# A hybrid attention layer: attention output kept once in fp32 and split at its load, the last branch product tile by tile, score banks opened before the staging buffers

## The chip, the cores and the metric

The kernel runs on one core of a Trainium2 chip. The metric is the device time of one execution in microseconds, over three runs: 1683.67, 1685.21 and 1689.54, median 1685.21. Engines are called as in the profile: PE (matmul), PEld (its weight load), DVE (vector), ACT (scalar), POOL (GpSimd) and SP, which issues every DMA of this kernel in one order.

## The reference

One layer of a backbone: 1024 latent tokens and 256 context tokens of width 1024 go through one combined projection and two branches, gated linear attention (a) and differential attention (b). The branches are gated, merged and projected.

```python
def diff_attention(q1, q2, k1, k2, v, lam):      # 8 heads, blocks of 128 queries
        s1 = jnp.einsum('bhqd,bhkd->bhqk', qb1, k1).astype(jnp.float32) * scale
        s2 = jnp.einsum('bhqd,bhkd->bhqk', qb2, k2).astype(jnp.float32) * scale
        a = jax.nn.softmax(s1, axis=-1) - lam * jax.nn.softmax(s2, axis=-1)
        return jnp.einsum('bhqk,bhkv->bhqv', a.astype(v.dtype), v)
...
    a = merge_heads(rms_norm(o_gla) * gla_gain) * jax.nn.silu(gla_gate)
    b = merge_heads(rms_norm(o_diff) * diff_gain * (1 - lam_init)) * jax.nn.silu(diff_gate)
    y = jax.nn.sigmoid(m_gla) * (a @ w_br_gla) + jax.nn.sigmoid(m_diff) * (b @ w_br_diff)
    return y @ w_out
```

All of it is fp32. The kernel reaches that precision with two tensors for one: `hi`, a copy in the reduced format fp32r, and `lo`, what is left of the value. A product of two such pairs is three matmuls (`mm3`, L340): hi·hi, hi·lo, lo·hi.

## The kernel before

**Order.** The program is recorded by Python coroutines. Class `Driver` holds modelled times of the engines and runs the coroutine that is due first by time and priority; what it emits is the fixed order of instructions of PE, ACT, DVE and POOL, and SP issues the DMAs in the order in which they were recorded. So an edit of one coroutine can change the order of others. Buffers have tags with a count (`TAGS`, L231): `acq` takes one, `rel` gives it back when an instruction is done. A tag lies in a pool, and pools are opened and closed by stage, the next on the place of the last.

**Stages in the profile.** Projections and linear attention, to about 911 us (PSUM tiles mm, tp and others); differential attention, 911 to 1485; the rest of the branch products, to about 1606; the output product, to 1682.3; the last stores, to 1685.9.

**Opening of attention.** `to_b` waits until the tiles of five tags are idle (mm and tp in PSUM; w aside, the staging tiles p, pl and rope in SBUF), closes psA and sbA and opens psW, psB and sbB, which hold the score banks and attention's SBUF tiles.

**Attention.** For a head and a block of 128 queries: scores into a PSUM tile `s` of five banks, maxima on DVE (TENSOR_REDUCE, into `sm`), exponentials on ACT (`att_exp`, into `e`), the mix of the two softmaxes on DVE, transposes on PE through one of two PSUM banks `b1` (in the profile `b<-ident,e`), copies to SBUF and splits (`at`), and the product with v (`b<-at,vv`). Once for a head and a pair of blocks, 32 times in all, `att_fin` normalises the output, transposes it into a `b1` bank (`pb`), and splits it there: `hi` by ACT, `lo` by DVE, both read the bank, and the bank is given back behind `lo`. The two halves take two SBUF tiles `b1k` of five and are stored to `d_bT[0]` and `d_bT[1]`. `b<-ident,b1k` is the transpose, `b1k<-b` ACT's hi, and `b1k<-b,b1k` with output type fp32r is DVE's lo; `b1k<-b,b1k` with type f32 is another instruction of `att_fin`, a product of the first transpose with the gate, and holds the other bank.

**Fill.** Beside all this, `fill` runs the products that need no attention: gates (kind 0), a @ w_br_gla (kind 1, 8 tiles), and at the end b @ w_br_diff (kind 2, 8 tiles, PSUM tiles `mc`). A tile is 128 output channels; its weights are loaded (`raw`), split into two of four `wt` buffers (ACT hi, DVE lo), and it runs in two halves of 512 tokens, 24 matmuls each (8 k times 3). The right-hand operands are 16 buffers `h0` for the first half and 16 `h1` for the second. Tiles go in pairs: (n, half 0), (n+1, half 0), (n, half 1), (n+1, half 1). When the last pair of kind 1 has ended half 0, its 16 h0 buffers are given back, and `loads` fetches the 16 tiles hi and lo of half 0 of b from `d_bT` into them; half 1 follows likewise. The first two tiles of kind 2 go through `first_two`, whose four half tiles have their own banks: for half 0 it takes each k of both tiles in turn.

**Output product.** `left`, `right` and `stream` compute y @ w_out with seven products of quarter size. Operands of the left side are formed from y's tiles (`ya`, `yb`, `yc`, `yf`), those of the right side from w_out (`wr`, then `h<-wr`, or sums in `raw`, then `h<-raw`). y's half tiles are finished by `post_y`: DVE multiplies the PSUM tile by a gate into `o` and adds the other branch into `yf`.

Of the kernel before, what the change touches and what calls it, by code (L numbers as in the profile page):

```python
# [10 lines left out]
F32 = mybir.dt.float32  # L11
F32R = mybir.dt.float32r
# [216 lines left out]
class Hybrid:  # L229
# [160 lines left out]
    def scratch(self):  # L390
# [10 lines left out]
        self.d_aT = [[d(f"d_aT{j}{h}", [2, P, S]) for h in range(4)] for j in range(2)]  # L401
        self.d_bT = [[d(f"d_bT{j}{i}", [P, S]) for i in range(8)] for j in range(2)]
        self.d_m = [[d(f"d_m{j}{i}", [P, S]) for i in range(8)] for j in range(2)]
# [1432 lines left out]
    def att_exp(self, u, comp, s5):  # L1836
# [3 lines left out]
        yield d.on("DVE", mx)  # L1840
        self.dve.tensor_scalar(mx, mx, u["mt"][:, comp:comp + 1], None, ALU.min)
        yield from self.acq("e5")
        E = u["E"][comp] = self.t("e5", [P, T])
# [123 lines left out]
    def att_fin(self, hd, pr, po, zs):  # L1967
# [35 lines left out]
        yield AtPE(e)  # L2003
        yield from self.acq("b1k", 2)
        yield from self.acq("b1")
        pb = self.t("b1", [P, 2, P])
        for x in range(2):
            e = self.tr(pb[:, x], oo[:, x])
        self.rel("b1k", e)
        yield On(e, "ACT")  # L2010
        hi = self.t("b1k", [P, 2, P], F32R)
        lo = self.t("b1k", [P, 2, P], F32R)
        e = yield from self.split2(pb, hi, lo, "b1", self.SF)
        self.store([(self.d_bT[j][hd][:, pr * 256:(pr + 1) * 256], b.rearrange("p x t -> p (x t)")) for j, b in
                    enumerate((hi, lo))], ("b1k", 2), ("fin", 1), ev=self.ev_bT[hd] if pr == 3 else None)
        if (hd, pr) == (7, 3):
            self.d.set(self.ev_att)

    def fill(self):
# [80 lines left out]
        def loads(src, ready, prio=2):  # L2100
# [12 lines left out]
            return r  # L2113

        def pace(i):
            return self.ev_u[min(63, int(i * self.PACE))]
# [4 lines left out]
        while n < len(todo):  # L2121
            kind = todo[n][0]
            two = [x for x in (n, n + 1) if x < len(todo) and todo[x][0] == kind]
            end = all(t[0] != kind for t in todo[n + 2:])
            if kind == 2 and todo[n][1] == self.DT[0]:
                yield self.ev_c
                yield from self.first_two(evs[n:n + 2], (lambda: (ws[n], ws[n + 1])), rhs)
                n += 2
                continue
            for half in range(2):  # L2130
# [4 lines left out]
                if end:  # L2135
                    self.rel(f"h{half}", e, 2 * NK)
                    if half == 0 and kind == 0:
                        nxt = loads(lambda j, k: self.d_aT[j][k // 2][k % 2], [now] * NK)
                    if half == 0 and kind == 1:
                        nxt = loads(lambda j, k: self.d_bT[j][k], self.ev_bT)  # L2140
            n += len(two)
# [4 lines left out]
    def first_two(self, evs, ws, rhs):  # L2146
# [4 lines left out]
        for x in range(4):  # L2151
            yield from self.acq("mc")
            pms.append(self.t("mc", [P, 512]))
        for ev in evs:
            yield ev[0]
        for x in range(4):
            d.spawn(self.load_y(self.DT[x // 2], x % 2), prio=-1)

        for half, k, m in [(0, k, m) for k in range(NK) for m in range(2)] + [(1, k, m) for m in range(2) for k in range(NK)]:
            yield rhs.ev[k, half]  # L2160
            hi, lo = ws()[m]
            e = self.mm3(pms[2 * m + half], hi[:, k], lo[:, k], rhs[0][k][half], rhs[1][k][half], k == 0, k == NK - 1)
# [6 lines left out]
    def phase_b(self):  # L2169
# [8 lines left out]
        def to_b():  # L2178
            yield self.ev_stream
            yield self.ev_b2  # L2180
            yield from self.idle("mm", "tp", "p", "pl", "rope")
            self.close("psA", "sbA")
            self.open("psW", "psB", "sbB")
            yield self.ev_b2
            d.set(self.ev_b)

        d.spawn(to_b(), prio=-3)
        self.ev_k, self.ev_v = [Event() for _ in range(8)], [Event() for _ in range(8)]
        for g in (self.att_keys, self.att_queries, self.att_values):
# [274 lines left out]
```

## Time and profile before

| | us |
|---|---|
| median of three runs | 1685.21 |
| span of the profiled execution (its own time) | 1685.9 |
| to 911: PE busy | 891.03 of 911.00 |
| 911 to 1485: PE busy | 555.13 of 574.00 |
| 1485 to 1534.7: PE busy | 48.02 of 49.70 |
| 1534.7 to 1682.3: PE busy | 147.60 of 147.60 |
| behind it: last stores | 3.60 |

A row of the timeline reads: start, duration, engine, line, operation, output <- inputs, shape, count, and in brackets the engine's idle time ahead of it with what ended it. A line of a helper stands for all its callers (L197 for ACT, DVE and POOL, L335 for matmuls, L361 for transposes), so groups are told apart by their tiles. In the table of stretches the columns are named in its first row; PEclk is the granted clock of PE as a share of full speed, and DMA the busy share of the 16 DMA engines.

### The profile page before, as it was taken

Reading aid. Unit: us, or ns where it says so; the run is one execution under the profiler, and the core shown is the slowest. Engines: PE = TensorE matmul, PEld = TensorE weight load, DVE = VectorE, ACT = ScalarE, POOL = GpSimd, SP = SyncE. Lnnn points to the kernel's source line nnn. Section 1 sums busy time; section 2 is a strip of 40 time slices with the busy share of each in tenths; the row PEclk is TensorE's granted clock in tenths of the full one; section 3 lists DMA queues with packets and bytes.
Section 4 is the critical chain, followed back from the end, with each engine's and each line's share of the span. In section 5 each row is a group of like instructions: output and inputs, shape, how many; then the busy total and the mean of one; then the engine's idle time right before and its main releaser. Section 6 shows DMA issues by size and latency. Waiting matters only on the chain.

```text
span 1685.9 us, 24403 instructions
## 1 busy us (share of the span) xinstructions
PE 1641.8 (97%) x8389; PEld 1358.3 (81%) x8389; DVE 1167.5 (69%) x2035; ACT 788.4 (47%) x1624; POOL 601.7 (36%) x649
## 2 busy tenths in 40 slices
PE   8999999999999999999999999999999999999999
PEld 3788788888788888888878888888888787887887
DVE  4797853455578697687762988787787887525694
ACT  4666423343334535455442665556666555411231
POOL 1500200000156475465530446555565555700000
PEclk9999999999999999999999999999999999999999
DMA  8557947687683665645375344345368552279422
GB/s 305 167 205 258 325 164 248 226 282 273 200 258 114 197 203 169 207 134 169 117 196 154 85 128 132 104 116 138 113 169 245 167 157 67 98 234 337 151 100 75
DMA packets 255884, 302.84 MB, mean 180 GB/s; under 512 B 21480, under 2 KB 173968, under 8 KB 255760
## 3 DMA queue, kind: packets, MB, share of 16 engines
q1 hardware_dynamic: 255760, 301.29, 56.9%
q8 instruction: 66, 1.08, 0.3%
q14 instruction: 58, 0.48, 0.1%
HBM read 203.71 MB, written 97.52 MB: 179 GB/s over the span
## 4 chain that ended last, share of the span: by engine, by line
PE 43%; DVE 6%; ACT 2%; DMA 2%; POOL 2%; issue 2%; ACTq 0%; DVEq 0%; POOLq 0%; SPq 0%
PE mc L335 10%; PE mm L335 7%; PE mb L335 7%; PE s L335 6%; PE b L335 5%; DVE sm L197 3%; PE b L361 3%; POOL at L197 2%; DVE e L197 2%; PE go L335 1%; ACT e L197 1%; DMA h<-d_bT 1%; PE mz L335 1%; PE gs L335 1%; PE tp L361 1%
## 5 line engine op out<-in xcount | busy, mean ns | idle before, releaser
L335 PE MATMUL mm<-w,h 128*128 128x512 f32 x1260 | 319.3, 402 | 0.6 <-DVE w L197 0.4
L335 PEld LDWEIGHTS mm<-w,h 128*128 128x128 f32 x1260 | 232.0, 189 | 48.0 <-issue 1.0
L197 DVE TENSOR_REDUCE sm<-s 128x1 f32<-128x1024 f32 (+1 forms) x192 | 194.4, 1037 | 49.0 <-PE s L335 47.4
L335 PE MATMUL mb<-h,wt 128*128 128x512 f32 x744 | 204.5, 407 | 2.5 <-ACT ft L197 2.1
L197 ACT ACTIVATE e<-s,sm 128x1280 f32<-128x1280 f32 x128 | 169.9, 1330 | 68.0 <-DVE sm L197 60.3
L197 POOL TENSOR_TENSOR at<-ac,at 128x512 fp32r<-128x512 f32 x128 | 184.7, 1443 | 10.7
L197 POOL TENSOR_SCALAR at<-ac 128x512 fp32r<-128x512 f32 x128 | 100.6, 786 | 236.0 <-ACT ac L197 166.9
L335 PE MATMUL s<-hk,aq 128*128 128x512 f32 (+1 forms) x768 | 178.2, 365 | 3.2 <-ACT e L197 1.1
L335 PEld LDWEIGHTS mb<-h,wt 128*128 128x128 f32 x744 | 131.1, 190 | 25.9 <-ACT ft L197 3.6
L335 PE MATMUL mc<-h,wt 128*128 128x512 f32 x600 | 141.2, 392 | 1.7 <-DMA h<-d_bT 0.8
L335 PE MATMUL mm<-h,w 128*128 128x512 f32 x576 | 139.4, 398 | 2.7 <-ACT p L197 1.1
L335 PEld LDWEIGHTS s<-hk,aq 128*128 128x128 f32 x768 | 122.3, 190 | 23.9 <-ACT e L197 5.1
L335 PEld LDWEIGHTS mc<-h,wt 128*128 128x128 f32 x600 | 111.3, 188 | 26.9 <-DMA h<-d_bT 3.3
L335 PE MATMUL b<-at,vv 128*128 128x256 f32 x960 | 130.6, 285 | 0.5 <-POOL at L197 0.4
L335 PEld LDWEIGHTS mm<-h,w 128*128 128x128 f32 x576 | 108.6, 191 | 27.0 <-DVE h L197 1.4
L335 PEld LDWEIGHTS b<-at,vv 128*128 128x128 f32 x960 | 122.7, 190 | 5.6 <-POOL at L197 1.2
L197 POOL TENSOR_TENSOR sm<-sm,nhalf 128x2 f32<-128x2 f32 (+2 forms) x94 | 106.1, 1129 | 53.6 <-DVE sm L197 48.1
L197 DVE TENSOR_TENSOR w<-raw,w 128x512 fp32r<-128x512 f32 x120 | 92.5, 789 | 31.5 <-ACT w L197 30.3
L197 ACT ACTIVATE ac<-b 128x512 f32<-128x512 f32 x120 | 71.1, 600 | 84.9 <-PE b L361 79.7
L197 DVE SCALAR_TENSOR_TENSOR e<-e,sm,e 128x1280 f32<-128x1280 f32 x64 | 108.7, 1698 | 0.6
L197 ACT ACTIVATE w<-raw 128x512 fp32r<-128x512 f32 x120 | 72.5, 628 | 70.3 <-DVE raw L197 22.8
L361 PE MATMUL b<-ident,e 128*128 128x128 f32 x598 | 92.5, 276 | 12.4 <-DVE at L197 4.3
(283 smaller groups left out, 2832.5 us busy)
## 6 DMA issues: line engine op xcount, KB each, us to landing
raw<-in_w_in SPq DMA_DIRECT2D x63, 512.0 KB, 4.7
g<-d_s SPq DMA_DIRECT2D x32, 640.0 KB, 5.2
aq<-d_qT SPq DMA_DIRECT2D x128, 128.0 KB, 3.4
d_dv<-pl SPq DMA_DIRECT2D x40, 256.0 KB, 2.2
gv<-d_v SPq DMA_DIRECT2D x40, 256.0 KB, 3.2
d_kT<-pl SPq DMA_DIRECT2D x40, 256.0 KB, 3.0
hk<-d_kT SPq DMA_DIRECT2D x32, 320.0 KB, 5.7
vv<-d_dv SPq DMA_DIRECT2D x16, 640.0 KB, 6.2
```

Source lines behind the costliest of these rows:

```text
L197: self.ins = f(out, *args, **kw).ins
L335: self.ins = self.nc.tensor.matmul(out, lhsT, rhs, start=start, stop=stop, skip_group_check=more).ins
L361: self.nc.tensor.transpose(out, src, self.ident[:n, :n])
```

## The change

1. `att_fin` copies the transposed output once, by ACT, into one fp32 tile `bb`, and gives the bank back behind that copy. One `b1k` buffer is taken instead of two, one store of 128 KB is made instead of two, and `d_bT` has 8 tensors instead of 16.
2. `splits` takes the place of `loads` for kind 2: each of 16 operand tiles is loaded as fp32 into a staging tile `wr` (8 buffers of pool sbC, so behind `ev_c2`, the event that says that sbC is open), then split by ACT and DVE into two h buffers.
3. Tiles 6 and 7 of kind 1 and all of kind 2 run one by one, half 0 and half 1 of a tile in turn. `first_two` takes k 0 to 6 of the first tile, k 0 to 6 of the second, then k 7 of both, and waits for each tile's weights apart.
4. `to_b` opens the score banks when mm and tp are idle; sbA is closed and sbB opened when p, pl and rope are idle too, and `att_exp` waits for that with a new event `ev_sb`.

By count PE has 8075 rows in both orders; DVE goes from 2026 to 2010, ACT from 1381 to 1397, SP from 1008 to 960; POOL has the same.

```diff
-        self.d_bT = [[d(f"d_bT{j}{i}", [P, S]) for i in range(8)] for j in range(2)]
+        self.d_bT = [d(f"d_bT{i}", [P, S]) for i in range(8)]
...
         self.dve.tensor_scalar(mx, mx, u["mt"][:, comp:comp + 1], None, ALU.min)
+        yield self.ev_sb
         yield from self.acq("e5")
...
-        yield from self.acq("b1k", 2)
+        yield from self.acq("b1k")
         yield from self.acq("b1")
         pb = self.t("b1", [P, 2, P])
...
-        hi = self.t("b1k", [P, 2, P], F32R)
-        lo = self.t("b1k", [P, 2, P], F32R)
-        e = yield from self.split2(pb, hi, lo, "b1", self.SF)
-        self.store([(self.d_bT[j][hd][:, pr * 256:(pr + 1) * 256], b.rearrange("p x t -> p (x t)")) for j, b in
-                    enumerate((hi, lo))], ("b1k", 2), ("fin", 1), ev=self.ev_bT[hd] if pr == 3 else None)
+        bb = self.t("b1k", [P, 2, P])
+        self.rel("b1", self.act.activation(bb, pb, AF.Copy))
+        self.store([(self.d_bT[hd][:, pr * 256:(pr + 1) * 256], bb.rearrange("p x t -> p (x t)"))],
+                   ("b1k", 1), ("fin", 1), ev=self.ev_bT[hd] if pr == 3 else None)
...
+        def splits():
+            r = Rhs([[[None] * 2 for _ in range(NK)] for _ in range(2)])
+            r.ev = {(k, half): Event() for k in range(NK) for half in range(2)}
+
+            def one(k, half, x):
+                yield from self.acq(f"h{half}", 2)
+                hi, lo = (self.t(f"h{half}", [P, 512], F32R) for _ in range(2))
+                r[0][k][half], r[1][k][half] = hi, lo
+                yield d.on("ACT", x)
+                self.act.activation(hi, x, AF.Copy)
+                yield d.on("DVE", hi)
+                e = self.dve.tensor_tensor(lo, x, hi.bitcast(F32), ALU.subtract)
+                self.rel("wr", e)
+                d.set(r.ev[k, half], e)
+
+            def run():
+                yield self.ev_c2
+                for half in range(2):
+                    for k in range(NK):
+                        yield self.ev_bT[k]
+                        yield from self.acq("wr")
+                        x = self.t("wr", [P, 512])
+                        self.dma(x, self.d_bT[k][:, half * 512:(half + 1) * 512])
+                        d.spawn(one(k, half, x), prio=-2)
+            d.spawn(run(), prio=-2)
+            return r
...
-            two = [x for x in (n, n + 1) if x < len(todo) and todo[x][0] == kind]
-            end = all(t[0] != kind for t in todo[n + 2:])
+            one = kind == 2 or todo[n][:2] in ((1, 6), (1, 7))
+            two = [n] if one else [n, n + 1]
+            end = all(t[0] != kind for t in todo[n + len(two):])
             if kind == 2 and todo[n][1] == self.DT[0]:
                 yield self.ev_c
-                yield from self.first_two(evs[n:n + 2], (lambda: (ws[n], ws[n + 1])), rhs)
+                yield from self.first_two(evs[n:n + 2], (lambda m: ws[n + m]), rhs)
...
-                        nxt = loads(lambda j, k: self.d_bT[j][k], self.ev_bT)
+                        nxt = splits()
...
-        for ev in evs:
-            yield ev[0]
-        for x in range(4):
-            d.spawn(self.load_y(self.DT[x // 2], x % 2), prio=-1)
-
-        for half, k, m in [(0, k, m) for k in range(NK) for m in range(2)] + [(1, k, m) for m in range(2) for k in range(NK)]:
+        order = [(0, k, m) for m in range(2) for k in range(NK - 1)] + [(0, NK - 1, 0), (0, NK - 1, 1)]
+        for half, k, m in order + [(1, k, m) for m in range(2) for k in range(NK)]:
+            yield evs[m][0]
+            if k == 0:
+                d.spawn(self.load_y(self.DT[m], half), prio=-1)
             yield rhs.ev[k, half]
-            hi, lo = ws()[m]
+            hi, lo = ws(m)
...
-            yield from self.idle("mm", "tp", "p", "pl", "rope")
-            self.close("psA", "sbA")
-            self.open("psW", "psB", "sbB")
-            yield self.ev_b2
+            yield from self.idle("mm", "tp")
+            self.close("psA")
+            self.open("psW", "psB")
             d.set(self.ev_b)
+            yield from self.idle("p", "pl", "rope")
+            self.close("sbA")
+            self.open("sbB")
+            d.set(self.ev_sb)
```

Where rows move. First DVE in attention, around the 22nd of the 32 splits: `sm<-s` are maxima, `b1k<-b,b1k` reads a `b1` bank (the fifth row is the lo, the last the product with the gate). Before:

```order
L197 TENSOR_REDUCE sm_13607<-s_1691_8527 128x1
L197 TENSOR_REDUCE sm_13606<-s_1691_8527 128x2
L197 TENSOR_REDUCE sm_13608<-s_1691_8527 128x1
L197 TENSOR_SCALAR sm_13607<-sm_13607,sm_13606 128x1
L197 TENSOR_TENSOR b1k_13684<-b_2842_13679,b1k_13683 128x256
L197 TENSOR_SCALAR sm_13608<-sm_13608,sm_13606 128x1
L197 TENSOR_TENSOR b1k_13667<-b_2845_13692,b1k_13667 128x256
```

Now:

```order
L197 TENSOR_REDUCE sm_13516<-s_1691_8515 128x1
L197 TENSOR_REDUCE sm_13515<-s_1691_8515 128x2
L197 TENSOR_REDUCE sm_13517<-s_1691_8515 128x1
L197 TENSOR_SCALAR sm_13516<-sm_13516,sm_13515 128x1
L197 TENSOR_SCALAR sm_13517<-sm_13517,sm_13515 128x1
L197 TENSOR_TENSOR b1k_13547<-b_2819_13567,b1k_13547 128x256
```

The lo is gone; the product still stands behind the three maxima.

Then PE where kind 2 begins (`mc` is the PSUM tile, `h` the operand, `wt` the weights; a new `wt` number is a new tile or its lo half). Before:

```order
L335 MATMUL mc_15526<-h_2752_13266,wt_15409 128x512
L335 MATMUL mc_15560<-h_3210_15472,wt_15533 128x512
L335 MATMUL mc_15560<-h_3211_15474,wt_15533 128x512
L335 MATMUL mc_15560<-h_3210_15472,wt_15534 128x512
L335 MATMUL mc_15562<-h_3210_15472,wt_15596 128x512
L335 MATMUL mc_15562<-h_3211_15474,wt_15596 128x512
```

Now, from the first tile's k 6 (18 matmuls into it):

```order
L335 MATMUL mc_15465<-h_3203_15431,wt_15368 128x512
L335 MATMUL mc_15465<-h_3204_15432,wt_15368 128x512
L335 MATMUL mc_15465<-h_3203_15431,wt_15369 128x512
L335 MATMUL mc_15467<-h_3191_15419,wt_15483 128x512
L335 MATMUL mc_15467<-h_3192_15420,wt_15483 128x512
```

The second tile's weights are used behind 21 matmuls of the first instead of behind 3. ACT now does there:

```order
L197 ACTIVATE h_3191_15419<-wr_15395 128x512
L197 ACTIVATE h_3193_15421<-wr_15397 128x512
L197 ACTIVATE h_3195_15423<-wr_15399 128x512
L197 ACTIVATE h_3197_15425<-wr_15401 128x512
L197 ACTIVATE h_3199_15427<-wr_15403 128x512
L197 ACTIVATE wt_15483<-raw_15285 128x1024
L197 ACTIVATE h_3203_15431<-wr_15407 128x512
L197 ACTIVATE h_3201_15429<-wr_15405 128x512
```

These are the operands' copies k 0 to 4, the second tile's weights, then k 6 and k 5; before, this stretch held weights alone.

Last, DVE where the output product's first operands are formed (`o<-o,mc` and `yf<-o` finish a half tile of y, `raw<-raw,gbo` and `h<-raw,h` form an operand). Before:

```order
L197 TENSOR_SCALAR o_16127<-o_16127,mc_16126 128x512
L197 TENSOR_TENSOR yf_16159<-o_16127 128x512
L197 TENSOR_TENSOR raw_15947<-raw_15947,gbo_15381 128x512
L197 TENSOR_TENSOR raw_16059<-raw_16059,gbo_15381 128x512 x2
L197 TENSOR_TENSOR h_3346_16169<-raw_15947,h_3345_16168 128x512
```

Now:

```order
L197 TENSOR_SCALAR o_16055<-o_16055,mc_16054 128x512
L197 TENSOR_TENSOR yf_16087<-o_16055 128x512
L197 TENSOR_SCALAR o_16090<-o_16090,mc_16089 128x512
L197 TENSOR_TENSOR yf_16118<-o_16090 128x512
L197 TENSOR_TENSOR raw_15875<-raw_15875,gbo_15247 128x512
L197 TENSOR_TENSOR raw_15952<-raw_15952,gbo_15247 128x512 x2
L197 TENSOR_TENSOR h_3333_16128<-raw_15875,h_3332_16127 128x512
```

One half tile more of y is finished ahead of the operands.

More of the change, by code (lines that the diff above doesn't have):

```diff
@@ L2180, in to_b @@
             yield self.ev_b2
-            yield from self.idle("mm", "tp", "p", "pl", "rope")
-            self.close("psA", "sbA")
-            self.open("psW", "psB", "sbB")
-            yield self.ev_b2
+            yield from self.idle("mm", "tp")
+            self.close("psA")
+            self.open("psW", "psB")
             d.set(self.ev_b)
+            yield from self.idle("p", "pl", "rope")
+            self.close("sbA")
+            self.open("sbB")
+            d.set(self.ev_sb)
         d.spawn(to_b(), prio=-3)
+        self.ev_sb = Event()
         self.ev_k, self.ev_v = [Event() for _ in range(8)], [Event() for _ in range(8)]
```

## The prediction, made before the changed kernel was run

> **What bounds the kernel now.** I read the page first, then the busy times by stage, then the tensor engine's waits and its timeline in the two stages that the change touches.
>
> ```profile
> span 1685.9 us, 24403 instructions
> PE 1641.8 (97%) x8389; PEld 1358.3 (81%) x8389; DVE 1167.5 (69%) x2035; ACT 788.4 (47%) x1624; POOL 601.7 (36%) x649
> ```
>
> PE works 97% of the span; every other engine has room on the average. So only three things can move the end: a gap of PE, a lowered clock, or a different number of matmuls. The change leaves that number as it is (8075 rows on PE in both orders), so I look for gaps and clock, stage by stage: attention, the tail of the branch products, the output product.
>
> ```profile
> core 0: us, PE busy (x) PEld busy (x) DVE busy (x) ACT busy (x) POOL busy (x), PEclk, DMA share, GB/s
> 911.00:1485.00 574.00, 555.13 (x3325) 474.02 (x3325) 445.61 (x857) 331.58 (x680) 312.62 (x288) 0.99 0.46 130
> 1485.00:1534.70 49.70, 48.02 (x206) 37.44 (x203) 10.82 (x13) 4.63 (x5) 0.00 (x0) 1.00 0.93 300
> 1534.70:1682.30 147.60, 147.60 (x650) 121.94 (x650) 108.38 (x167) 38.62 (x62) 0.00 (x0) 1.00 0.44 147
> ```
>
> The output product (last row) has PE busy in all of it: nothing to gain, only to lose. Attention leaves PE idle for 574.00 − 555.13 = 18.9 us. In the tail DVE and ACT have little to do and DMA is nearly full (0.93). The waits of PE in attention, by what ended them (us in total, times, longest):
>
> ```profile
> engine line waited for: us in total, times, longest us
> PE b L361 <- DVE at L197: 4.3, 6, 1.6
> PE b L361 <- DVE sm L197: 3.4, 1, 3.4
> PE b L361 <- DVE b1k L197: 3.1, 5, 2.0
> ```
>
> The longest two, with what DVE did just before them:
>
> ```profile
> 1339.98 2.94 DVE L197 TENSOR_REDUCE sm<-s 128x1 f32<-128x1024 f32 x3
> 1342.96 0.41 DVE L197 TENSOR_TENSOR b1k<-b,b1k 128x256 fp32r<-128x256 f32 x1
> 1343.42 0.41 DVE L197 TENSOR_TENSOR b1k<-b,b1k 128x256 f32<-128x256 f32 x1
> 1343.52 0.85 PE L361 MATMUL b<-ident,e 128*128 128x128 f32 x6 [3.35 <-DVE sm L197]
> ...
> 1409.12 0.42 DVE L197 TENSOR_TENSOR b1k<-b,b1k 128x256 fp32r<-128x256 f32 x1
> 1409.69 0.45 PE L361 MATMUL b<-ident,e 128*128 128x128 f32 x1 [2.03 <-DVE b1k L197]
> ```
>
> The instruction with the fp32r output is the lo half of att_fin's split. It reads a PSUM bank b and is what gives that bank back. Both gaps end some 0.15 us after it (1342.96 + 0.41 to 1343.52; 1409.12 + 0.42 to 1409.69): PE stood because the two b1 banks were held, one by a lo queued behind three REDUCEs. The row "DVE sm" names the wrong instruction for the first. Each gap is followed by a lower granted clock, the eighth column:
>
> ```profile
> 1344.00:1350.00 6.00, 5.98 (x27) 4.80 (x26) 3.88 (x9) 4.08 (x9) 5.11 (x7) 0.72 0.34 113
> 1410.00:1420.00 10.00, 10.00 (x53) 8.28 (x51) 8.06 (x16) 6.59 (x13) 5.94 (x6) 0.85 0.19 67
> ```
>
> **Part 1: attention output kept as one fp32 tensor.** It takes 32 lo subtractions from DVE (13.3 us) and leaves the 32 ACT copies as they are, with another output type:
>
> ```profile
> L197 DVE TENSOR_TENSOR b1k<-b,b1k 128x256 fp32r<-128x256 f32 x32 | 13.3, 414 | 4.9 <-ACT b1k L197 4.9
> L197 ACT ACTIVATE b1k<-b 128x256 fp32r<-128x256 f32 x32 | 12.3, 385 | 28.2 <-PE b L361 26.8 <-DMA aq<-d_qT 1.0
> ```
>
> DVE's 13.3 us lie beside PE and are worth nothing by themselves; what counts is that a bank now returns after the ACT copy. The gaps ended by a lo are 3.35 and 2.03, and one of 0.20 at 1019 that I leave at that; their clock losses are 6.00 × (1 − 0.72) = 1.7 and 10.00 × (1 − 0.85) = 1.5. Upper bound of the gain: 3.35 + 2.03 + 1.7 + 1.5 = 8.6 us. Lower bound 0: at 1343.42 the other bank was held too, by the product b1k<-b,b1k (f32 output) that still sits behind the same REDUCEs in the changed order, so that the same wait could end 0.3 us later by another owner. I take half, **−4.3**, since one of the two banks is free early in either gap, but the order around them is written anew. One long gap with its clock costs 3.35 + 1.7 = 5.1; a reordering can add one as well as remove one, so the range gets ±5 here. The stores fall from 64 to 32 beside a DMA share of 0.46: 0.
>
> A rule speaks on the clock. The Trainium skill, "TensorE: Matmul & The Clock Gate", section "HAM oscillation — how this bites in real kernels", asks for no idle gaps of PE above about 3.4 us, so by it neither gap here would cost clock. The trace disagrees: gaps of 3.35 and 2.03 us stand ahead of clocks of 0.72 and 0.85, and the measurement decides. By the rule the removable sum would be 5.4 instead of 8.6, half of it 2.7, and the whole forecast 1.6 us later.
>
> **Part 2: the split at the load, and the tail tile by tile.** What the tail loses now:
>
> ```profile
> 1485.00 30.89 PE L335 MATMUL mc<-h,wt 128*128 128x512 f32 x135
> 1516.13 0.73 PE L335 MATMUL mc<-h,wt 128*128 128x512 f32 x2 [0.24 <-ACT wt L197]
> 1517.39 14.01 PE L335 MATMUL mc<-h,wt 128*128 128x512 f32 x59 [0.53 <-DVE wt L197]
> 1531.56 0.73 PE L335 MATMUL mc<-h,wt 128*128 128x512 f32 x2 [0.16 <-DMA h<-d_bT]
> 1532.58 1.77 PE L335 MATMUL mc<-h,wt 128*128 128x512 f32 x4 [0.29 <-DMA h<-d_bT]
> 1534.68 25.68 PE L335 MATMUL mc<-h,wt 128*128 128x512 f32 x112 [0.33 <-DMA h<-d_bT]
> 1534.68 82.35 PE mc L335 x362
> ```
>
> The last row, of the chain of waits, gives the undisturbed price: 82.35 / 362 = 0.2275 us a matmul. The first five runs of the timeline are 135 + 2 + 59 + 2 + 4 = 202 matmuls, 45.95 us at that price, and take 1534.68 − 1485.00 = 49.68: **3.7 us lost**, to weights that become ready late (1516, 1517) and to operands still landing (1531 to 1534). The weights:
>
> ```profile
> 1515.02 1.06 ACT L197 ACTIVATE wt<-raw 128x1024 fp32r<-128x1024 f32 x1 [4.38 <-PE mc L335]
> 1516.11 1.23 DVE L197 TENSOR_TENSOR wt<-raw,wt 128x1024 fp32r<-128x1024 f32 x1 [4.21 <-ACT wt L197]
> h<-d_bT SPq DMA_DIRECT2D x32, 256.0 KB, 6.1
> L197 ACT ACTIVATE h<-wr 128x512 fp32r<-128x512 f32 x8 | 5.0, 625 | 6.7 <-PE mb L335 6.5
> L197 DVE TENSOR_TENSOR h<-wr,h 128x512 fp32r<-128x512 f32 x8 | 5.5, 686 | 0.4 <-PE mb L335 0.4
> ```
>
> Removed: 32 loads of 256 KB (8.4 MB in a stage that moves 49.7 us × 300 GB/s = 14.9 MB). Added: 16 loads of 256 KB, 16 ACT copies of 0.625 (10.0 us) and 16 DVE subtractions of 0.686 (11.0 us), prices from the same forms elsewhere. ACT has 49.70 − 4.63 = 45 us free and DVE 39, POOL takes no part: they hide if they come in time. First half: five operands are split while the last branch tile's second half runs (24 × 0.2275 = 5.46 us; five copies 3.1 and the last subtraction 0.7 behind). When that tile ends, ACT does the second tile's weights, 1.06, then k6, k5, k7, 0.625 each; DVE follows: weights lo at 1.06 + 1.23 = 2.3, then k5 at 3.0, k6 at 3.7, k7 at 4.4. Needed: k5's lo by the 17th matmul, 16 × 0.2275 = 3.6; k6's 4.3; k7's after two times 21 matmuls, 9.6; the second tile's weights after 21, 4.8 (before: after 3, 0.7, and that is the wait of 1516). Every one is ready, two by only 0.6 us; without this cover each us that ACT or DVE is late is a us of PE. The loads may wait in staging tiles ahead of the buffers' release, so the operands' landing leaves the path. Bounds of the gain 0 to 3.7; I take **−3.4**, near the top, as 0.3 is left for a first load or weight still late.
>
> **Part 3: score banks opened early.** All engines' rows, and what each waits for, are the same in both orders at the opening and for some hundred PE rows behind it. The first score matmul
>
> ```profile
> 911.31 2.58 PE L335 MATMUL s<-hk,aq 128*128 128x512 f32 x12 [0.74 <-ACT p L197]
> ```
>
> keeps its wait on ACT's last p. The most that could be had is this 0.74, the most that can be lost is nothing, as no wait is added ahead of it: **0**.
>
> **Part 4: the output product's start.** Single tiles change the order in which half tiles end, so that before the output product's first operands DVE now finishes four half tiles' gates and sums where it finished three.
>
> ```profile
> 1605.98 11.04 PE L335 MATMUL mc<-h,ya 128*128 128x512 f32 x48
> 1606.10:1617.00 10.90, 10.90 (x50) 9.03 (x49) 10.83 (x19) 2.70 (x5) 0.00 (x0) 1.00 0.49 156
> 1617.00:1627.90 10.90, 10.90 (x50) 9.03 (x49) 9.78 (x17) 4.78 (x10) 0.00 (x0) 1.00 0.20 74
> 1627.90:1638.80 10.90, 10.90 (x50) 9.03 (x49) 10.72 (x18) 4.56 (x10) 0.00 (x0) 1.00 0.06 24
> 1600.85 0.68 DVE L197 TENSOR_TENSOR h<-raw,h 128x512 fp32r<-128x512 f32 x1
> ```
>
> DVE is full in the first pieces, with 0.07 + 1.12 + 0.18 = 1.4 us to spare in 33. Its last subtraction for these operands, the row at 1600.85, lies 4.5 us ahead of the first matmul; the extra work puts DVE some 5 us further behind, so that this cover is used up. Counted through the order, the first operand comes about 1 us ahead of its use, the next product's last about 1 us ahead or none. Bounds 0 and 2.6 (5 less the spare, less a us of margin); I take **+0.3**.
>
> **The sum.** −4.3 − 3.4 + 0 + 0.3 = −7.4. The profiled execution's span is 1685.9, the median of the runs 1685.21, closer than the 5.9 us over which those scatter; from the median this gives 1677.8, forecast **1678**. A measurement of this kernel tells 0.3% (5.1 us) from no change: faster is below 1680.2, slower above 1690.3.
>
> **The rivals.**
> - *The tail's gain alone.* In attention the bank held by the product f32 b1k<-b,b1k takes over both waits. For it: at 1343.42 it was the second holder, and 4.3 us of the listed waits, under "DVE at", come from other DVE work. Against it: PE needs one bank to go on, and the copy frees it early. 1685.2 − 3.4 + 0.3 = 1682; the same. Chance 0.22.
> - *The slower side: attention's new order makes more bank waits.* Without 32 lo's DVE puts its REDUCEs and products elsewhere; products still wait behind REDUCEs (0.98 each, the row at 1339.98), while 150 instead of 132 matmuls of fill remain when attention ends, so less fill was spent in covering gaps. Two more gaps like that at 1343.52 cost 2 × 5.1 = 10.1, with −3.4 of the tail 1692. It decides once PE's idle in attention is above 18.9 + 3.4. Chance 0.15.
> - *The backlog of DVE decides at the output product.* 2.6 us late instead of 0.3 there: 1680.2 or later, the same. Chance 0.05.
> - *The splits come late in the tail.* The 0.6 us of cover is gone if ACT takes copies in another turn or a load lands late; the 3.4 stay lost: 1681.2, and 1686 if a wait of 4.4 us, all the splits behind the last tile's end, is added. Chance 0.04.
>
> My forecast has 0.54, of it 0.50 below 1680.2 and 0.04 above. So faster 0.50; same 0.04 + 0.22 + 0.05 + 0.03 and 0.01 of the slower case, 0.35; slower 0.15. Its own range is 1672 to 1682. The whole range is **1671 to 1688**: below, the sum with 8.6 − 4.3 more and some for a removed gap elsewhere; above, the rivals but for the worse part of the slower one.
>
> **What will show it.** In the profile after: no PE wait in attention that ends with a b1k of DVE in fp32r, PE idle there near 14 and clocks of 1.00 around the former gaps; about 46 us for 202 tail matmuls, with no wait for h or wt above 0.3; the first s<-hk still behind ACT p; no wait for h in the output product. A total wait of PE in attention above 22 us proves part 1 wrong; a tail that still loses 3 us proves part 2 wrong.

## The result, and the profile after

The changed kernel takes 1675.18 us, the median of 6 runs (1673.55 to 1676.87); the kernel before, beside it, 1687.47 (6 runs, 1683.67 to 1689.54). The ratio is 0.993, with a 95% interval of 0.9914 to 0.9946: faster by 0.7%.

The head of the page of the changed kernel, and the busy times of the same stretches as before (of each, the columns of the table before):

```profile
span 1675.2 us, 24268 instructions
PE 1634.8 (98%) x8389; PEld 1354.1 (81%) x8389; DVE 1166.3 (70%) x2019; ACT 796.3 (48%) x1640; POOL 606.4 (36%) x649
```

```profile
911.00:1485.00 574.00, 559.12 (x3352) 477.15 (x3351) 436.86 (x828) 330.93 (x681) 315.85 (x288) 1.00 0.44 127
1485.00:1534.70 49.70, 49.70 (x221) 41.14 (x220) 27.56 (x40) 15.70 (x24) 0.00 (x0) 1.00 0.91 302
```

DVE and ACT are busier in the second stretch, as the splits now lie there (27.56 and 15.70 us), and PE has no gap in it. Of PE's timeline three places: attention's first score product, the first matmul behind attention, the first of the output product.

```profile
910.12 2.58 PE L335 MATMUL s<-hk,aq 128*128 128x512 f32 x12 [0.74 <-ACT p L197]
...
1474.07 121.33 PE L335 MATMUL mc<-h,wt 128*128 128x512 f32 x534
1595.23 11.04 PE L335 MATMUL mc<-h,ya 128*128 128x512 f32 x48
```

The row of 534 matmuls is one run without a wait; the next starts 121.16 us later, so a matmul costs 121.16 / 534 = 0.2269 us, of which the tables below use 0.2268. With that price the two profiles can be set side by side. Attention ends with more or less fill left to do (516 matmuls before, 534 now), so I add the price of what is left to the time from the first score product to the last transpose, and call that *attention at equal fill*. What the branch products behind attention take above their price is the *tail's loss*.

| place | before | after | difference |
|---|---|---|---|
| start of attention | 911.31 | 910.12 | −1.2 |
| attention at equal fill | 573.69 + 117.03 = 690.7 | 563.95 + 121.11 = 685.1 | −5.7 |
| tail's loss | 120.98 − 117.03 = 3.95 | 121.16 − 121.11 = 0.05 | −3.9 |
| from the output product's start to the end of the span | 79.9 | 80.0 | 0 |

Together −10.7, the difference of the spans; by the medians, taken beside each other, it is −12.3. The first row isn't the change's: the order up to there is the same, and over the profiles of this study it starts between 907.05 and 911.31. PE's waits in attention are now these:

```profile
PE s L335 <- ACT e L197: 4.2, 9, 1.2
PE b L361 <- DVE at L197: 3.5, 6, 0.9
PE b L361 <- ACT b1k L197: 1.7, 6, 0.4
PE b L361 <- DVE b1k L197: 1.3, 4, 0.6
```

The long gaps of 3.35 and 2.03 us are gone; score products now wait nine times for ACT's exponentials instead of three times. All listed waits from 911 to 1468 sum to 13.9 us, before to 18.2. The granted clock gains too: before, three of the 20 us slices of attention have 0.91, 0.97 and 0.95, a loss of 20 × 0.17 = 3.4 us; now every slice has 1.00.

### The profile page after: what moved, and what is told of

Read it like the earlier page. It is cut to its first block, busy times and chain, and to the rows that moved or that the text cites. A ratio compares the mean times of both kernels' runs of the same rounds, so it can differ in the third digit from the quotient of the medians.

```text
span 1675.2 us, 24268 instructions
## 1 busy us (share of the span) xinstructions
PE 1634.8 (98%) x8389; PEld 1354.1 (81%) x8389; DVE 1166.3 (70%) x2019; ACT 796.3 (48%) x1640; POOL 606.4 (36%) x649
## 4 chain that ended last, share of the span: by engine, by line
PE 43%; DVE 7%; ACT 3%; issue 2%; POOL 1%; DMA 1%; SPq 0%; ACTq 0%; DVEq 0%; POOLq 0%
PE mc L335 11%; PE mm L335 7%; PE mb L335 7%; PE s L335 6%; PE b L335 5%; DVE sm L197 4%; PE b L361 3%; ACT e L197 2%; DVE e L197 2%; PE go L335 1%; POOL at L197 1%; PE mz L335 1%; PE gs L335 1%; PE tp L361 1%; PE gt L335 1%
## 5 line engine op out<-in xcount | busy, mean ns | idle before, releaser
L197 POOL TENSOR_TENSOR at<-ac,at 128x512 fp32r<-128x512 f32 x128 | 191.2, 1493 | 10.7
L335 PEld LDWEIGHTS s<-hk,aq 128*128 128x128 f32 x768 | 120.5, 189 | 27.2 <-ACT e L197 11.7
L335 PE MATMUL mc<-h,wt 128*128 128x512 f32 x600 | 137.7, 390 | 0.0
L197 POOL TENSOR_TENSOR sm<-sm,nhalf 128x2 f32<-128x2 f32 (+2 forms) x94 | 102.3, 1089 | 26.0 <-DVE sm L197 20.8
L197 POOL TENSOR_TENSOR p<-p,gdif 128x512 f32<-128x512 f32 x12 | 16.2, 1359 | 242.6 <-DMA d_dv<-pl 194.6
```

Of the source, the lines that this page charges most:

```text
L197: self.ins = f(out, *args, **kw).ins
L335: self.ins = self.nc.tensor.matmul(out, lhsT, rhs, start=start, stop=stop, skip_group_check=more).ins
```

## The experiments

Each run was timed in five rounds beside the kernel before, whose median stayed at 1687.4. Attention and tail are from one profile of each, with the price above; "listed waits" are PE's from 911 to 1468. Profiles of one order differ among themselves: the changed kernel and run 6 have the same order on every engine and 685.1 and 684.2, runs 1 and 5 the same order up to the tail and 693.3 and 691.0. So 1 to 2 us between two profiles prove little.

| run | median | ratio, 95% | attention at equal fill | listed waits | tail's loss |
|---|---|---|---|---|---|
| before | 1687.4 | | 690.7 | 18.2 | 3.95 |
| changed kernel | 1675.2 | 0.9914 to 0.9946 | 685.1 | 13.9 | 0.05 |
| 1 fp32 and split alone | 1693.1 | 1.0024 to 1.0043 | 693.3 | 19.7 | 9.0 |
| 2 tiles alone | 1692.6 | 1.0017 to 1.004 | 690.5 | 17.0 | 10.8 |
| 3 bank held | 1685.4 | 0.9979 to 0.9999 | 694.6 | 21.4 | 0.05 |
| 4 bank free | 1683.1 | 0.9956 to 0.9981 | 691.8 | 18.7 | 0.05 |
| 5 no re-queueing | 1683.9 | 0.9971 to 0.9994 | 691.0 | 18.2 | 0.05 |
| 6 re-queueing, old opening | 1674.5 | 0.9913 to 0.9943 | 684.2 | 13.7 | 0.06 |
| 7 before without lo | 1685.0 | 0.9974 to 0.9994 | 690.2 | 16.0 | 4.0 |
| 8 first two k by k | 1676.3 | 0.9918 to 0.995 | 684.1 | 13.7 | 1.4 |
| 9 opening alone | 1687.6 | 0.999 to 1.0017 | 690.6 | 16.8 | 4.6 |
| 10 re-queued in att_fin too | 1671.5 | 0.9881 to 0.9915 | 679.0 | 10.5 | 0.06 |
| 11 re-queued elsewhere | 1691.7 | 1.0012 to 1.0036 | 701.3 | 25.2 | 0.05 |
| 12 tiles in pairs | 1682.2 | 0.9955 to 0.9977 | 684.2 | 13.7 | 6.7 |

**1. The fp32 output and the split alone.** The first two parts of the change; pairs, k by k and opening as before.

```diff
+        bb = self.t("b1k", [P, 2, P])
+        self.rel("b1", self.act.activation(bb, pb, AF.Copy))
...
+                        nxt = splits()
```

> The kernel before with only the fp32 attention output and the split at its load; tiles still in pairs, the first two of the last product still k by k, score banks opened as before. Theory: attention gains by itself, some 5 us (as the changed kernel's trace has it: 5.6 less in attention at equal fill), and the tail gains only the part that waited for loads, 1 to 2 of its 3.9 us, because the second tile's weights are still used 3 matmuls behind the first's: about 7 us below before, ratio 0.996. Rival, that the tile-by-tile order carries the tail alone: 5 us below before with the tail losing 3.9 as before. Rival, that attention's gain comes from the new order at the opening: within 0.2% of before.

Slower, by 5.7 us, where about 7 faster was expected. Neither half of the theory held: attention gained nothing (693.3 against 690.7), and the tail lost 9.0 instead of less than before. PE and ACT at that place in the timeline:

```profile
1470.76 45.17 PE L335 MATMUL mc<-h,wt 128*128 128x512 f32 x198
1522.41 7.92 PE L335 MATMUL mc<-h,wt 128*128 128x512 f32 x24 [6.49 <-ACT wt L197]
```

```profile
1510.59 2.18 ACT L197 ACTIVATE h<-wr 128x512 fp32r<-128x512 f32 x4
1513.03 2.69 ACT L197 ACTIVATE h<-wr 128x512 fp32r<-128x512 f32 x4 [0.26 <-DMA wr<-d_bT]
1518.88 1.27 ACT L197 ACTIVATE h<-wr 128x512 fp32r<-128x512 f32 x2 [3.16 <-DMA wr<-d_bT]
1520.79 0.63 ACT L197 ACTIVATE h<-wr 128x512 fp32r<-128x512 f32 x1 [0.64 <-DMA wr<-d_bT]
1521.32 1.04 ACT L197 ACTIVATE wt<-raw 128x1024 fp32r<-128x1024 f32 x1
```

The second tile's weights (the last ACT row) stand behind eleven splits in ACT's order, and those wait for their own loads. PE needs the weights 3 matmuls into the product and stands 6.49 us, then runs 24 matmuls in 7.92 instead of 5.4, at a granted clock of 0.63 (1522.4 to 1528).

**2. The tile order alone.** Part three of the change, with hi and lo still stored and loaded apart.

```diff
+            one = kind == 2 or todo[n][:2] in ((1, 6), (1, 7))
+            two = [n] if one else [n, n + 1]
...
+        order = [(0, k, m) for m in range(2) for k in range(NK - 1)] + [(0, NK - 1, 0), (0, NK - 1, 1)]
```

> The kernel before with only the tile-by-tile order of the last tiles and the new order in the first two; hi and lo still stored and loaded apart. Theory: the order alone hurts, because the operand buffers of half 0 come free 24 matmuls (5.5 us) ahead instead of 48 (10.9), and 16 loads of 256 KB at 300 GB/s take 14 us to land: PE waits 4 to 8 us more for them at the start of the last branch product, ratio 1.002 to 1.005. Rival, that the tile-by-tile order gains by itself: the tail's loss falls from 3.9 to below 2, ratio 0.998 to 0.999. Attention and the output product as before under both.

As the theory had it: 5.2 us slower, all of it in the tail (10.8 lost, 6.9 more than before), waiting for the loads:

```profile
1513.36 1.15 PE L335 MATMUL mc<-h,wt 128*128 128x512 f32 x3 [0.99 <-DMA h<-d_bT]
1515.32 1.40 PE L335 MATMUL mc<-h,wt 128*128 128x512 f32 x3 [0.81 <-DMA h<-d_bT]
...
1535.79 74.15 PE L335 MATMUL mc<-h,wt 128*128 128x512 f32 x317 [0.97 <-DMA h<-d_bT]
```

Yet the listed waits there sum to 4.0 us only. The larger part is the granted clock, 0.87, 0.91 and 0.83 in these three stretches, where the kernel before has 1.00:

```profile
1505.00:1520.00 15.00, 12.34 (x45) 8.40 (x43) 2.51 (x3) 1.06 (x1) 0.00 (x0) 0.87 0.99 319
1520.00:1535.00 15.00, 14.48 (x56) 10.43 (x54) 3.36 (x5) 0.63 (x1) 0.00 (x0) 0.91 1.02 352
1535.00:1545.00 10.00, 9.21 (x32) 6.94 (x33) 3.42 (x5) 2.06 (x3) 0.00 (x0) 0.83 0.78 261
```

By them 15 × 0.13 + 15 × 0.09 + 10 × 0.17 = 5.0 us go to the clock, an estimate.

So each half of the tail's edit costs 5 to 7 us by itself, and both together gain 3.9.

**3 and 4. The bank and DVE's work, in one order.** In the changed kernel 32 subtractions are put back on DVE without the knowledge of the planner (class `Driver`), so that every other instruction keeps its place. In run 3 they read the transposed output in its PSUM bank, in run 4 the copy in SBUF. The result is read by nobody.

```diff
-        self.rel("b1", self.act.activation(bb, pb, AF.Copy))
+        e = self.act.activation(bb, pb, AF.Copy)
+        self.rel("b1", e)
+        def extra():
+            self.nc.vector.tensor_tensor(self.xx, pb, bb, ALU.subtract)   # run 4: bb, bb
+            return
+            yield
+        self.d.spawn(extra(), On(e, "DVE"), prio=-10)
```

> The changed kernel with one more DVE subtraction for each of the 32 attention outputs, reading the transposed output in its PSUM bank as the removed lo did (into a tile that nobody reads; the order of all other instructions on every engine is the changed kernel's). Theory, the bank: PE's waits in attention grow by 3 to 8 us, ended by this subtraction, and the time is 1679 to 1683. Rival, DVE's load: the same rise here and in the run that reads SBUF. Rival, the order: within 1 us of the changed kernel's 1675.2, as the order is the same and the place of the held bank is covered.

> The same 32 extra DVE subtractions at the same places in the same order, but reading the fp32 copy in SBUF, so that the bank is given back by ACT as in the changed kernel. Theory, the bank: 1675 to 1676.5, PE's waits in attention as in the changed kernel (14 us of them). Rival, DVE's load (13 us more of it): as slow as the run with the bank held, 1679 to 1683. Rival, the order: within 1 us of 1675.2 here too.

Both theories get a share; both times lie at or above the top of the range of 1679 to 1683. Without holding the bank the subtractions add 6.7 us to attention (691.8 against 685.1; medians, 1683.1 against 1675.2); holding it adds 2.8 more (2.4 by the medians). Which share is the larger isn't shown, as the two runs load DVE unequally. Run 4's subtractions take 21.1 us of it, run 3's 13.3, as the removed lo did:

```profile
L2019 DVE TENSOR_TENSOR xx<-b1k 128x256 fp32r<-128x256 f32 x32 | 21.1, 660 | 5.2 <-ACT b1k L197 5.1
```

```profile
L2019 DVE TENSOR_TENSOR xx<-b,b1k 128x256 fp32r<-128x256 f32 x32 | 13.3, 416 | 5.5 <-ACT b1k L197 5.3
```

Of PE's waits, run 4 and then run 3:

```profile
PE s L335 <- ACT e L197: 8.3, 12, 1.5
```

```profile
PE b L361 <- DVE xx L2019: 7.5, 9, 1.5
PE s L335 <- ACT e L197: 4.7, 9, 1.1
```

In run 4 the waits for exponentials double from 4.2 to 8.3; in run 3 nine waits end with the extra subtraction itself (`xx`).

**5 and 6. The re-queueing.** The fourth edit moves nothing at the opening, but it puts a wait into `att_exp`. When the event is long set, that wait still hands the coroutine back to the planner's queue, 128 times. Run 5 takes only this away, run 6 keeps only this, with the opening as before. An order that the planner happens to emit is called a draw below.

```diff
+        if self.ev_sb.t is None:      # run 5, in place of the bare wait
+            yield self.ev_sb
...
+        yield self.ev_b               # run 6; to_b as before
```

The order of run 6 is the changed kernel's on every engine; that of run 5 is run 1's up to the tail.

> The changed kernel, score banks still opened early, but a coroutine of att_exp waits for the staging buffers' event only while it isn't set; once it is set the coroutine goes on at once, where the changed kernel puts it back into the planner's queue. This makes the order in attention that of the run with the fp32 split alone; opening and tail are the changed kernel's. Theory, the order in attention is set by that re-queueing and carries the gain there: attention as in that run, some 8 us longer than in the changed kernel at equal fill, the tail without loss, 1682 to 1685. Rival, attention was long in that run for another reason (its tail, or chance): 1674 to 1677.

> The counterpart: fp32 split and tile order as in the changed kernel, the opening as before (all five tags idle, one event), and in att_exp one wait for the opening's own event, which is always set there, so that only the re-queueing is left of the fourth edit. The order on all engines is the changed kernel's. Theory, re-queueing: the changed kernel's time within 1 us, 1674 to 1676.5. Rival, the early opening itself is worth something: slower by what it is worth, 1 us or more.

The theory held twice. With the early opening and without the re-queueing attention takes 691.0, as before; with the re-queueing and the old opening 684.2. By the medians the order is worth 9.4 us (1683.9 to 1674.5), and the early opening nothing that these runs can tell. PE's waits of run 5, to be held against those of the changed kernel:

```profile
PE s L335 <- ACT e L197: 6.1, 13, 1.2
PE b L361 <- ACT ac L197: 4.8, 6, 1.2
PE b L361 <- DVE at L197: 2.8, 4, 1.2
```

Nothing stands out as one place: four more waits for exponentials, and ACT's copies of transposed probabilities (`ac`) late six times instead of two. The granted clock is 1.00 in every slice of attention here as well, so the clock isn't what parts the two orders.

**7. The kernel before, its order kept, without the 32 lo.** The planner still counts them, but they aren't emitted; hi is stored in both places, so that the last product takes it twice (so the output lacks the precision of lo).

```diff
-        e = yield from self.split2(pb, hi, lo, "b1", self.SF)
+        yield On(self.act.activation(hi, pb, AF.Copy), "DVE")
+        e = self.d.op("DVE", 0.07 + 256 * 0.00104, [lo], [pb, hi.bitcast(F32)])
+        self.rel("b1", e)
```

> The kernel before with its own order of all instructions, but the 32 lo subtractions of the attention output are left out (hi is stored in the place of lo, so the output lacks that precision); the bank is given back behind ACT's hi. Theory, DVE's work and the held bank cost PE time in attention whatever the order: attention 6 to 10 us shorter, as 32 subtractions made it 6.7 (bank free) and 9.5 (bank held) longer in the changed kernel's order; 1678 to 1682. Rival, only the gaps that a lo ended go: at most 8.6 with clock, near 4, 1683. Rival, the gain came from the new order alone: within 1 us of before, 1687.5. The tail loses 3.9 as before under all.

The theory fell: 2.4 us by the medians (1.0 to 4.4 by the interval), 0.5 in attention by the profile. The rival of the gaps was nearest in the time, but the gaps didn't go. At the place of the longest gap of before, DVE and PE:

```profile
1335.29 2.94 DVE L197 TENSOR_REDUCE sm<-s 128x1 f32<-128x1024 f32 x3
...
1338.40 0.41 DVE L197 TENSOR_TENSOR b1k<-b,b1k 128x256 f32<-128x256 f32 x1
```

```profile
1338.87 1.12 PE L361 MATMUL b<-ident,e 128*128 128x128 f32 x4 [2.94 <-DVE b1k L197]
```

```profile
1338.90:1345.00 6.10, 6.10 (x19) 4.88 (x20) 3.53 (x10) 4.13 (x8) 4.74 (x6) 0.50 0.33 111
```

The gap is there without the lo, 2.94 instead of 3.35 us. Four transposes now run ahead of it (at 1335.33), as a bank is free, and it ends with the product (type f32) that holds the other bank behind the same three REDUCEs. The granted clock behind it is 0.50 for 6 us. The second gap is there too, 2.01 instead of 2.03 us; it now ends with another instruction of DVE, the one that frees the fill's PSUM tile `mb`:

```profile
1405.79 0.96 PE L335 MATMUL mb<-h,wt 128*128 128x512 f32 x3 [2.01 <-DVE ft L197]
```

```profile
1405.00:1415.00 10.00, 9.21 (x45) 7.92 (x46) 7.96 (x17) 5.79 (x12) 5.19 (x5) 0.83 0.23 79
```

The profile hides a part of the gain. Its listed waits are 2.2 us less than before, but in the 20 us slices of attention its clock loses 20 × (0.17 + 0.09 + 0.01 + 0.07) = 6.8 us against 3.4.

**8. The first two tiles k by k again**, all else as changed.

```diff
-        order = [(0, k, m) for m in range(2) for k in range(NK - 1)] + [(0, NK - 1, 0), (0, NK - 1, 1)]
+        for half, k, m in [(0, k, m) for k in range(NK) for m in range(2)] + [(1, k, m) for m in range(2) for k in range(NK)]:
```

> The changed kernel with the first two tiles of the last branch product taken k by k again, so that the second tile's weights are used 3 matmuls behind the first's; the tiles are still single and the split is at the load. Theory: a wait for those weights of 1.06 + 1.23 less 0.7, near 1.6 us, comes back at that place, and nothing else: 1676.5 to 1678. Rival, the order of these two tiles is covered anyway: 1675.2.

1676.3, 0.2 below the range of the theory and 1.1 above the changed kernel; the tail loses 1.4, where 1.6 was worked out, at the weights alone:

```profile
1507.12 0.73 PE L335 MATMUL mc<-h,wt 128*128 128x512 f32 x2 [0.24 <-ACT wt L197]
1508.38 86.22 PE L335 MATMUL mc<-h,wt 128*128 128x512 f32 x379 [0.53 <-DVE wt L197]
```

**9. The opening and its wait alone, on the kernel before.**

```diff
-            yield from self.idle("mm", "tp", "p", "pl", "rope")
+            yield from self.idle("mm", "tp")
...
+        yield self.ev_sb
```

> The kernel before with only the fourth edit: score banks opened early, and the re-queueing wait in att_exp. Each engine's rows are those of the kernel before, operation by operation (a few buffers trade names). Theory: the edit acts through the order alone, and here the order doesn't change: the time of before, ratio 0.999 to 1.001, the first score matmul still behind ACT's p. Rival, the early opening has a worth of its own: 1 us or more below before.

No difference (0.999 to 1.0017), and the first score product waits 0.74 us for ACT's p as ever. The same re-queueing that changes the order with the fp32 output changes no operation's place with the old one.

**10 and 11. Other draws of the order.** A wait on a long set event is put at other places, the changed kernel otherwise: in run 10 at the start of `att_fin`, that in `att_exp` kept; in run 11 at the starts of `att_fin` and `att_split` in its stead. The instructions are the same.

```diff
+        yield self.ev_b               # run 10: att_fin; run 11: att_fin and att_split
```

> The changed kernel with one more re-queueing wait, at the start of att_fin (on an event that is long set; the wait for the staging buffers in att_exp is kept beside it). The same instructions, in another order in attention. Theory, the order in attention is a draw worth several us either way: at equal fill attention differs from the changed kernel's by more than 1 us; this is the best of the draws by the planner's own model, 1670 to 1674. Rival, the changed kernel's order is good for a reason that other orders share, its fewer DVE instructions and earlier banks: within 1 us of 1675.

> The changed kernel with the re-queueing wait at the start of att_fin and of att_split in place of att_exp: the same instructions, and by the planner's own model the worst of the draws. Theory, the order is a draw: 1680 to 1688, all of the gain in attention gone, the tail without loss. Rival, the fewer DVE instructions carry the gain: within 2 us of 1675.

1671.5, as the theory had it, and 1691.7, beyond its 1688: 20 us apart, and by the profiles the difference is attention (679.0 and 701.3). Run 10 is faster than either kernel. Its profile is the fastest of its six runs, 3.4 us below their median, so 679.0 flatters it. PE's longest groups of waits, run 10 and run 11:

```profile
PE b L361 <- DVE at L197: 4.6, 7, 0.9
PE b L361 <- ACT ac L197: 1.5, 2, 0.8
...
PE s L335 <- ACT e L197: 0.7, 3, 0.3
```

```profile
PE s L335 <- ACT e L197: 7.2, 10, 1.5
PE b L361 <- DVE at L197: 4.5, 6, 1.5
PE b L361 <- DVE b1k L197: 4.1, 10, 0.7
```

Score products behind exponentials wait 0.7 us in the one and 7.2 in the other. Both profiles have a granted clock of 1.00 in every slice of attention.

**12. The last tiles in pairs**, the first two of the last product in the new order, all else as changed.

```diff
-            two = [n] if one else [n, n + 1]
+            two = [x for x in (n, n + 1) if x < len(todo) and todo[x][0] == kind]
```

> The changed kernel with its last tiles in pairs again; the first two tiles of the last product keep the new order (7 k of the one, 7 of the other). ACT's order then has all 16 splits of the operands ahead of the second tile's weights. Theory: PE waits for these weights behind splits that wait for their own loads, as in the run with the fp32 split alone (9.0 us lost there with the weights needed 4.1 us earlier): 4 to 6 us lost in the tail, 1679 to 1681. Rival, the order of the first two tiles suffices: 1675 to 1676.

As the theory had it, somewhat worse: 6.7 lost in the tail, 1682.2. PE, and the granted clock behind its gap:

```profile
1516.40 0.73 PE L335 MATMUL mc<-h,wt 128*128 128x512 f32 x2 [4.13 <-ACT wt L197]
1517.66 22.53 PE L335 MATMUL mc<-h,wt 128*128 128x512 f32 x92 [0.53 <-DVE wt L197]
```

```profile
1516.40:1521.00 4.60, 4.07 (x11) 2.97 (x12) 1.21 (x1) 0.00 (x0) 0.00 (x0) 0.63 0.94 331
```

The waits are 4.7 us, and some 4.07 × (1 − 0.63) = 1.5 more of PE's busy time go to the clock.

## Why the prediction was right, and where it was not

The forecast was 1678, the time is 1675.2: inside the range and on the right side. Its sum of −7.4 stands against −10.7 by the profiles, of which −1.2 lies ahead of the change, and −12.3 by the medians; the forecast time came out nearer than the gain because it was counted from 1685.21, and the kernel before, timed beside the changed one, took 1687.47. And one term came out near by luck, for a reason that was wrong.

**Part 2, −3.4: right in size and in reason.** Measured −3.9. The tail has no wait left, the operands' landing left the path (run 2 shows what it costs when it stays), and the second tile's weights moved from 3 to 21 matmuls behind the first's (run 8: 1.4). What I had not seen is that the two edits need each other: single tiles alone, run 2, and the split alone, run 1, each lose more than before. "Without this cover each us that ACT or DVE is late is a us of PE" is run 12: there the splits stand ahead of the weights, and 6.7 us go.

**Part 1, −4.3: near the measured −5.7, and wrong in its mechanism.** The step that failed is "I take half, −4.3, since one of the two banks is free early in either gap". In run 7 the lo is away, the order is kept, and a bank is free early; yet both gaps are there, 2.94 and 2.01 us in place of 3.35 and 2.03, and PE stands for the other bank in the one and for the fill's tile in the other. The lower bound's reason, that the same wait ends by another owner, is what happens. Of what run 7 gains all the same, 0.5 us in attention by its profile and 2.4 by the medians, these two gaps give 0.4. Run 5, with the fp32 output and the bank given back by ACT but without the re-queueing, takes 691.0, as before.

The signs that the forecast named beforehand all came: no wait for an fp32r b1k of DVE, PE idle for 574.00 − 559.12 = 14.9 us in attention, and a clock of 1.00 at the former gaps. They couldn't tell the missing lo from a new order in which these gaps don't arise; only the runs that hold one of the two could.

**Part 3, 0: the other step that failed.** "All engines' rows, and what each waits for, are the same in both orders at the opening and for some hundred PE rows behind it" was true and the opening is worth nothing (runs 6 and 9). But I stopped reading there. The edit's new wait in `att_exp` changes the planner's draw in attention further on, and this, on top of the fp32 output, is what gains: 691.0 to 684.2 (runs 5 and 6). It needs the fp32 output with its split, since on the kernel before the same wait moves no operation (run 9). The forecast allowed ±5 for an order "written anew"; runs 10 and 11, chosen as the best and the worst by the planner's own model, show the draw to be wider, −6.0 and +16.3 from the changed kernel.

**"DVE's 13.3 us lie beside PE and are worth nothing by themselves"** is near the truth in the order of before (run 7) and false in the new one, where 32 subtractions that hold no bank, though with 21.1 us of DVE, cost 6.7 (run 4), and 32 that hold it, with 13.3, cost 9.5 (run 3). With them the new order takes 694.6, more than the 690.7 of before: neither the order nor the missing lo gains by itself what both gain together. Why DVE's time counts in the new order is argued only: late maxima would delay the exponentials that free the score banks, and this fits run 4, where ACT's exponentials wait 60.9 us for maxima instead of 50.0 and PE's waits for `e` double, but it was not tried apart.

**Part 4, +0.3: 0.** The output product runs from its start without a wait. The estimate of the cover was close: DVE's subtraction for the last of its first operands ends about 1.0 us after the product's first matmul, where it is needed 2.27 after.

```profile
1595.54 0.69 DVE L197 TENSOR_TENSOR h<-raw,h 128x512 fp32r<-128x512 f32 x1
```

**The rivals.** "The tail's gain alone" is right for the longer gap in what it says of the product that takes over the wait (run 7), and its price of 1682 is near run 5's 1683.9. "More bank waits in the new order", 1692, is what another draw gives (run 11, 1691.7), though there the largest group of waits is for exponentials, 7.2 of 25.2 us. "The splits come late" is runs 1 and 12.

**The clock.** The forecast set the rule of the Trainium skill ("TensorE: Matmul & The Clock Gate", section "HAM oscillation — how this bites in real kernels"; gaps above about 3.4 us) against two gaps below it. Run 7 adds 2.94 us, with a clock of 0.50 behind it. The measurement decides against the rule as a limit here. But the length of a gap doesn't decide alone: run 2 has the order of before in attention and the same gap, 3.34 us, and the clock behind it is 1.00 (1340 to 1350).

What stays open: whether the fp32 output is worth anything in attention over all orders. Four orders with it gave 679.0, 684.2, 691.0 and 701.3, the order without it 690.7; that is a spread, not a gain. Open too: what the missing lo is worth in the order of before, between the 0.5 of the profile and the 4.4 at the end of the medians' interval.

## What to carry to other kernels

Where a planner draws the order, an edit has two effects: what it does, and the order it draws. Measure the second by itself: hold the order and put the work back or take it away (runs 3, 4, 7), and redraw the order with the work unchanged (5, 10, 11); here the second was the larger, ±10 us against 3.9. Two edits that each lose can gain together, so test a bundle's parts alone and together before keeping or dropping one. And compare orders to the end of the stage, not only at the place of the edit.

## What the runs showed of the hardware

A microsecond of listed waits of PE in attention goes with about one and a half of time: from run 10 to run 11 the waits rise by 14.7 us (10.5 to 25.2) and attention by 22.3 (679.0 to 701.3; the medians differ by 20.2). PE's idle time in attention rises by 15.0 of them (11.7 to 26.7). The other 7.3 lie in PE's busy time for the same number of matmuls, and not in the clock, which is 1.00 throughout in both; what they are isn't shown.

The granted clock falls behind gaps of quite different length: 0.72 over 6 us after 3.35, 0.50 over 6.1 after 2.94, 0.63 over 4.6 after 4.13, 0.85 over 10 after 2.03. One gap of 2.0 us in attention has a lowered clock behind it in all four profiles of that order (before and runs 2, 7 and 9: 0.85 over 10 us in the first, 0.83 in the others), while the one of 3.34 us has none in run 2. In run 2's tail the clock falls to 0.87 and 0.83 though no listed wait there is above 0.99 us.
